# Two-layer decoder trunk on one core: the residual stream is laid out with tokens on partitions, and the out and down projections stream 512 weight columns

## The chip, the core and the metric

The kernel runs on one core of a Trainium2 chip. The core has five engines that run their own instruction streams and meet at semaphores: TensorE (PE, with its weight loads shown as PEld), VectorE (DVE), ScalarE (ACT), GpSimd (POOL) and SyncE (SP), which here issues DMAs. The metric is the device time of one execution in microseconds.

## What is computed

A trunk of two layers over 256 tokens of 1024 channels, all in float32. Each layer normalizes, mixes tokens in three ways, adds to the residual stream x, normalizes again, runs a gated MLP with a short convolution over positions, and adds to x; a closing norm ends it.

```python
D_MODEL = 1024; SEQ = 256; DEPTH = 2; D_FF = 2816

def rms_norm(x, g):
    y = xf * lax.rsqrt(jnp.mean(xf * xf, axis=-1, keepdims=True) + RMS_EPS)
    return y.astype(x.dtype) * g
...
    for i in range(DEPTH):
        h = rms_norm(x, norm_mix_g[i])
        x = x + hybrid_mixer(h, ..., w_branch[i], b_gate[i], w_out[i])
        h = rms_norm(x, norm_ffn_g[i])
        x = x + conv_ffn(h, w_up[i], ffn_conv_w[i], ffn_conv_b[i], w_down[i])
    return rms_norm(x, norm_f_g)
```

The two products that write the residual stream are the out projection (1024 x 1024 weights, the end of `hybrid_mixer`) and the down projection (2816 x 1024, the end of `conv_ffn`).

## The kernel before

**Float32 as two parts.** Every operand is split into a high part in a reduced format (fp32r) and the low rest; a product is three TensorE products, high x high, low x high and high x low, added up in PSUM. Activations are split by `split_scaled` (L290): ScalarE writes the high part times the norm's gain (L292), VectorE the low part (L293), into `slot_h` and `slot_l`.

**Weights.** They come from memory in 302 pieces, most of 128 x 1024 numbers (512 KB). `piece` (L157) loads one (L166, on SyncE's queue, four raw buffers), ScalarE casts it to `whi` (L173), VectorE subtracts to get `wlo` (L174); six buffers hold the two parts, and pieces are prepared `LOOK` = 5 ahead of their use. A dictionary `before` holds other loads that go into SyncE's queue ahead of a piece.

**Main stream and side tasks.** `stream()` runs the layers; the large products follow one another on TensorE, and a generator gives way after each step of some products. The token mixers and the factor of a norm are side tasks: `spawn` starts one, and it says how many steps of the main stream to wait before it goes on (the tables `N` and `W`). The framework's scheduler then fixes the order on each engine.

**Residual stream.** `xT` is [128, 8, 256]: channel 128 k + p of all tokens is row p of block k. A product that writes it has 128 weight columns as the stationary operand and streams the 256 tokens: `chan_steps` (L207; products at L217 to L219) for the out projection, `add_down` (L946; L954 to L956) for the down projection, which runs `FFN_LAG` = 3 tiles behind the up projection. Four PSUM banks `dacc` collect the down projection over its 22 tiles of 128 hidden channels. `take` (L914) and `add_x` (L979) add a bank to `xT` on VectorE. As soon as two blocks of `xT` are new, `Norm.part` splits them for the next product and squares them (L309), and GpSimd adds up the squares (L311).

**A norm's factor.** The factor of a token, 1 / rms, isn't needed for the next product, only for what takes its result. `Norm.factor` adds the squares' halves on GpSimd (L320), sums over channels by four products of TensorE with a single streamed column (L324), does a Newton iteration of small operations on VectorE (`rsqrt`, L271), makes a diagonal matrix `dg` (L331), and spreads it over partitions by another product (L334) into `r_bc`.

**Closing norm.** `Final` (L339) squares each pair of blocks when it is done (L349), adds them up (L351, L358), sums over channels on TensorE (L362), iterates (L274 to L279), spreads the factor (L369, L370), and scales the eight blocks on VectorE (L372), with five output DMAs (L376).

## Time and profile before

| | |
|---|---|
| median of 3 runs | 946.69 us (945.66 to 948.6) |
| span of the profiled execution | 946.7 us |
| TensorE busy | 931.4 us, 7258 products |
| VectorE busy | 715.4 us |
| ScalarE busy | 511.2 us |
| GpSimd busy | 96.5 us |
| moved by DMA | 165.45 MB, mean 175 GB/s |

Times are microseconds from the start of the span. A busy TensorE isn't necessarily a TensorE at its peak: its products are pipelined, and a product's shown duration is longer than the step from its start to that of the next. The step is what a product costs in a stream of products. An idle time in brackets names what ended it.

### The profile page before, as it was taken

What the parts mean: (1) busy time and instruction counts of PE and PEld (TensorE: products, weight loads), DVE (VectorE), ACT (ScalarE), POOL (GpSimd) and SP (SyncE); (2) the same over time, 40 slices, a digit from 0 to 9 for tenths busy, and PEclk for the clock granted to TensorE, in tenths of its full rate; (3) what the DMA queues carried; (4) which work ended last, traced back from release to release, by engine and by line L of the source; (5) the groups of instructions that cost most, each with busy time, mean ns of one, the idle gap of its engine ahead of it and who ended that gap; (6) DMA issues with size and microseconds to landing.
All of it is one profiled execution on the core that took longest, in us unless ns stands there. A gap on an engine that the chain in (4) does not pass through costs nothing.

```text
span 946.7 us, 18084 instructions
## 1 busy us (share of the span) xinstructions
PE 931.4 (98%) x7258; PEld 897.3 (95%) x7258; DVE 715.4 (76%) x1105; ACT 511.2 (54%) x755; POOL 96.5 (10%) x88
## 2 busy tenths in 40 slices
PE   8999999999999999999999999999999999999995
PEld 8899899899999999999999998989999999999995
DVE  6986888575578877777799578877657897777775
ACT  6665454554466555555557645544544575555541
POOL 3022200002120000000022031000202200000000
PEclk9999999999999999999999999999999999999998
DMA  7674665445565656665456556545565666666521
GB/s 236 215 230 130 233 187 164 142 153 180 172 196 166 200 179 181 182 189 183 145 181 183 171 166 216 154 149 147 173 189 169 181 193 182 182 187 188 178 91 45
DMA packets 49428, 165.45 MB, mean 175 GB/s; under 512 B 5760, under 2 KB 8384, under 8 KB 49344
## 3 DMA queue, kind: packets, MB, share of 16 engines
q1 hardware_dynamic: 49056, 163.90, 56.6%
q8 instruction: 57, 0.93, 0.4%
q10 hardware_dynamic: 288, 0.39, 0.1%
q14 instruction: 27, 0.22, 0.1%
HBM read 161.12 MB, written 1.05 MB: 171 GB/s over the span
## 4 chain that ended last, share of the span: by engine, by line
PE 92%; DMA 2%; DVE 2%; ACT 2%; issue 1%; SPq 0%; DVEq 0%; ACTq 0%
PE mm L217 21%; PE mm L218 20%; PE mm L219 20%; PE mx L955 4%; PE mx L954 4%; PE mx L956 4%; PE mm L264 4%; PE mm L265 4%; PE mm L266 3%; DMA raw<-w_all 2%; PE mx L486 2%; ACT whi L173 1%; PE mx L489 1%; DVE wlo L174 1%; PE mx L473 1%
## 5 line engine op out<-in xcount | busy, mean ns | idle before, releaser
L217 PE MATMUL mm<-slot_h,whi 128*128 128x256 f32 x1696 | 484.4, 286 | 1.4 <-ACT slot_h L292 1.4
L218 PE MATMUL mm<-slot_l,whi 128*128 128x256 f32 x1696 | 481.3, 284 | 0.6 <-DVE slot_l L293 0.6
L219 PE MATMUL mm<-slot_h,wlo 128*128 128x256 f32 x1696 | 481.0, 284 | 0.0
L174 DVE TENSOR_TENSOR wlo<-raw,whi 128x1024 fp32r<-128x1024 f32 (+1 forms) x300 | 376.0, 1255 | 113.3 <-ACT whi L173 109.9
L173 ACT CAST whi<-raw 128x1024 fp32r<-128x1024 f32 (+1 forms) x302 | 311.2, 1033 | 262.5 <-PE mm L218 163.0
L217 PEld LDWEIGHTS mm<-slot_h,whi 128*128 128x128 f32 x1696 | 326.2, 193 | 4.1 <-ACT slot_h L292 2.1
L218 PEld LDWEIGHTS mm<-slot_l,whi 128*128 128x128 f32 x1696 | 326.5, 193 | 1.5 <-DVE slot_l L293 1.2
L219 PEld LDWEIGHTS mm<-slot_h,wlo 128*128 128x128 f32 x1696 | 326.4, 192 | 0.1
L954 PE MATMUL mx<-slot_h,whi 128*128 128x256 f32 x346 | 97.9, 283 | 0.0
L955 PE MATMUL mx<-slot_l,whi 128*128 128x256 f32 x346 | 97.9, 283 | 0.0
L956 PE MATMUL mx<-slot_h,wlo 128*128 128x256 f32 x346 | 97.9, 283 | 0.0
L937 DVE SCALAR_TENSOR_TENSOR tm<-tm,par 128x254 f32<-128x254 f32 (+1 forms) x176 | 73.8, 477 | 0.7 <-ACT tm L935 0.7
L954 PEld LDWEIGHTS mx<-slot_h,whi 128*128 128x128 f32 x346 | 66.4, 192 | 0.0
L955 PEld LDWEIGHTS mx<-slot_l,whi 128*128 128x128 f32 x346 | 66.4, 192 | 0.0
L956 PEld LDWEIGHTS mx<-slot_h,wlo 128*128 128x128 f32 x346 | 66.4, 192 | 0.0
L264 PE MATMUL mm<-whi,slot_h 128*128 128x512 f32 x160 | 63.5, 397 | 0.2 <-DVE tm L408 0.2
L265 PE MATMUL mm<-wlo,slot_h 128*128 128x512 f32 x160 | 63.1, 394 | 0.0
L266 PE MATMUL mm<-whi,slot_l 128*128 128x512 f32 x160 | 62.5, 392 | 0.0
L935 ACT ACTIVATE tm<-tm,par 128x256 f32<-128x256 f32 x88 | 48.2, 593 | 4.1 <-DVE tm L930 4.0
L930 DVE TENSOR_TENSOR tm<-mm,r_bc 128x512 f32<-128x512 f32 x44 | 30.4, 690 | 22.1 <-PE mm L219 22.1
L941 ACT CAST slot_h<-tm 128x256 fp32r<-128x256 f32 x44 | 17.8, 406 | 50.7 <-DVE tm L940 50.7
L311 POOL TENSOR_TENSOR sqacc<-sqacc,tm 128x512 f32<-128x512 f32 x12 | 17.3, 1441 | 234.8 <-ACT tm L309 234.5
(197 smaller groups left out, 784.0 us busy)
## 6 DMA issues: line engine op xcount, KB each, us to landing
raw<-w_all SPq DMA_DIRECT2D x292, 512.0 KB, 3.6
st<-ret_decay SPq DMA_DIRECT2D x8, 384.0 KB, 4.1
raw<-w_all SPq DMA_DIRECT2D x10, 256.0 KB, 4.6
xT<-x_t SPq DMA_DIRECT2D x4, 256.0 KB, 7.0
r_c<-q SPq DMA_DIRECT2D x16, 64.0 KB, 2.1
r_d<-q SPq DMA_DIRECT2D x16, 64.0 KB, 2.1
r_a<-phases SPq DMA_DIRECT2D x2, 256.0 KB, 4.1
out_dram<-xT SPq DMA_DIRECT2D x2, 256.0 KB, 2.0
```

Of the source, the lines that this page charges most:

```text
L173: nc.scalar.copy(h_out, r_in)
L174: nc.vector.tensor_tensor(l_out, r_in, h_out.bitcast(F32), ALU.subtract)
L217: nc.tensor.matmul(o, lhsT=wh[:, c], rhs=ah[:, k, :], start=first, stop=False)
L218: nc.tensor.matmul(o, lhsT=wh[:, c], rhs=al[:, k, :], start=False, stop=False)
L219: nc.tensor.matmul(o, lhsT=wl[:, c], rhs=ah[:, k, :], start=False, stop=last)
L264: nc.tensor.matmul(acc[t], lhsT=ah[:, k, c], rhs=wh, start=first, stop=False)
L265: nc.tensor.matmul(acc[t], lhsT=ah[:, k, c], rhs=wl, start=False, stop=False)
L266: nc.tensor.matmul(acc[t], lhsT=al[:, k, c], rhs=wh, start=False, stop=last)
L937: nc.vector.scalar_tensor_tensor(a[:, d:], u[:, :T - d], mx.pc("fconv_w", 3 * ct + 2 - d), a[:, d:], ALU.mult, ALU.add)
L954: nc.tensor.matmul(o, lhsT=wh[:, c], rhs=ah[:, a, :], start=(first and i == 0), stop=False)
L955: nc.tensor.matmul(o, lhsT=wh[:, c], rhs=al[:, a, :], start=False, stop=False)
L956: nc.tensor.matmul(o, lhsT=wl[:, c], rhs=ah[:, a, :], start=False, stop=end)
```

## The change

The residual stream becomes `xt`, [128, 2, 1024]: token 128 t + p is row p of token tile t. The out projection (`tok_major`, one half of 512 channels after the other) and the down projection (`add_down` by half c and token tile t) now have 128 tokens of the activations as the stationary operand and stream 512 weight columns. Per layer that is 96 products for the out projection in place of 192, and 264 for the down projection in place of 528. The weights of the out projection lie in memory in another order for this.

The sum of squares of a token now lies along its row: `grow` adds a half bank to `xt` and squares it with ScalarE's accumulator (`ss`). No sums over partitions are left except in layer 0's first norm (`FirstNorm`), which still loads a channel-major copy of x into two borrowed buffers. The next product, though, needs channels on partitions, so `TokNorm.turn` transposes a half on TensorE (eight 128 x 128 blocks) into PSUM and splits from there. `DOWN_END` and `CLOSE_END` give the order of the last entries of the down projection (tiles from the end, half, token tile). The closing norm multiplies by a broadcast gain (on GpSimd for three of the four quarters, on VectorE for the last), iterates for each token tile, and scales along rows. New loads are x by tokens (1 MB, ahead of an early piece) and the gain of the closing norm (512 KB, in layer 1).

The core of the diff (comments and the packing of inputs left out):

```diff
FFN_LAG = 3
-DOWN_LAG = 2.5
+DOWN_END = ((3, 0, 0), (2, 0, 0), (3, 0, 1), (2, 0, 1), (3, 1, 0), (2, 1, 0), (1, 0, 0), (1, 0, 1),
+            (3, 1, 1), (2, 1, 1), (1, 1, 0), (1, 1, 1))
+CLOSE_END = ((3, 0, 0), (2, 0, 0), (3, 1, 0), (2, 1, 0), (4, 0, 1), (3, 0, 1), (1, 0, 0), (1, 1, 0),
+             (4, 1, 1), (3, 1, 1), (2, 1, 1), (2, 0, 1), (1, 0, 1), (1, 1, 1))
...
 REST = 9
...
-N = (3, 8, 4, 5, 1)
+N = (3, 8, 3, 5, 3, 2)
...
+X_AT = 40
...
-    def tok_major(l, kind, act):
+    def tok_major(l, kind, act, half=0):
         ah, al = act
         acc = [mm_tile() for _ in range(2)]
         for k in range(KT):
-            wh, wl = weight(l, kind, k // 4, k % 4, 512)
+            wh, wl = weight(l, kind, 2 * half + k // 4, k % 4, 512)
             for t in range(2):
                 c = slice(t * P, (t + 1) * P)
                 first, last = k == 0, k == KT - 1
...
     class Norm:
         def __init__(self, g, slot):
             self.g, self.slot = g, slot
+            self.r_bc = None
+        def spread(self, src):
+            r = rsqrt(src, 2, 1.0 / D, 1e-6)
+            rh = sm.tile([P, 2], F32, name="rh", tag="rh")
+            nc.vector.tensor_scalar(rh, r, 0.5, None, ALU.mult)
+            dg = sm.tile([P, T], F32, name="dg", tag="sq1", bufs=1)
+            for t in range(2):
+                nc.vector.tensor_scalar(dg[:, t * P:(t + 1) * P], ident, r[:, t:t + 1], None, ALU.mult)
+            yield self.late
+            pb = mx_tile()
+            nc.tensor.matmul(pb[:, :T], lhsT=ones[:, :P], rhs=dg, start=True, stop=True)
+            r_bc = sm.tile([P, T], F32, name="r_bc", tag="r_bc", bufs=1)
+            nc.scalar.copy(r_bc, pb[:, :T])
+            self.r, self.rh, self.r_bc = r, rh, r_bc
+    class FirstNorm(Norm):
+        late = N[1]
+        def __init__(self, g, slot):
+            super().__init__(g, slot)
             self.acc = sm.tile([P, 512], F32, name="sqacc", tag="sqacc", bufs=1)
-            self.r_bc = None
-        def split(self, j):
-            for k in (2 * j, 2 * j + 1):
-                split_scaled(self.slot[0][:, k, :], self.slot[1][:, k, :], xT[:, k, :], self.g[:, k:k + 1])
+            self.x = [mix.tile([P, 4, T], F32, name="x_t", tag=q) for q in ("m_lo", "m_hi")]
+        def ahead(self, j):
+            o = 2 * (j % 2)
+            x = self.x[j // 2][:, o:o + 2, :]
+            nc.sync.dma_start(x, xT_in[:, 2 * j:2 * j + 2, :])
+            for i in range(2):
+                k = 2 * j + i
+                split_scaled(self.slot[0][:, k, :], self.slot[1][:, k, :], x[:, i, :], self.g[:, k:k + 1])
         def square(self, j):
             sq = self.acc if j == 0 else t_main()
-            nc.scalar.activation(two(sq), xT[:, 2 * j:2 * j + 2, :], AF.Square)
+            o = 2 * (j % 2)
+            nc.scalar.activation(two(sq), self.x[j // 2][:, o:o + 2, :], AF.Square)
             if j:
                 nc.gpsimd.tensor_tensor(self.acc, self.acc, sq, ALU.add)
-        def part(self, blocks):
-            j = blocks[0] // 2
-            self.split(j)
-            self.square(j)
         def factor(self):
             s1 = sm.tile([P, T], F32, name="sq1", tag="sq1", bufs=1)
...
             for t in range(2):
                 nc.tensor.matmul(pv[:, t:t + 1], lhsT=s1[:, t * P:(t + 1) * P], rhs=ones[:, 0:1],
                                  start=(t == 0), stop=(t == 1))
...
+            yield from self.spread(pv[:, 0:2])
+    def grow(ss, c, t, acc):
+        x = xt[:, t, 512 * c:512 * c + 512]
+        nc.vector.tensor_tensor(x, x, acc, ALU.add)
+        sq = t_main()
+        nc.scalar.activation(sq, x, AF.Square, accum_out=ss[:, 2 * c + t:2 * c + t + 1])
+        return x
+    class TokNorm(Norm):
+        late = N[4]
+        def __init__(self, g, slot):
+            super().__init__(g, slot)
+            self.ss = sm.tile([P, 4], F32, name="xss", tag="xss")
+        def add(self, c, t, acc):
+            grow(self.ss, c, t, acc)
+        def turn(self, c):
+            for q in (2 * c, 2 * c + 1):
+                pt = mx_tile()
+                for j in range(2):
+                    for t in range(2):
+                        nc.tensor.transpose(pt[:, j * T + t * P:j * T + (t + 1) * P],
+                                            xt[:, t, (2 * q + j) * P:(2 * q + j + 1) * P], ident)
+                for j in range(2):
+                    k = 2 * q + j
+                    split_scaled(self.slot[0][:, k, :], self.slot[1][:, k, :], pt[:, j * T:(j + 1) * T],
+                                 self.g[:, k:k + 1])
+        def turn_late(self, c):
+            self.turn(c)
+            yield 1
+        def factor(self):
+            s2 = sm.tile([P, 2], F32, name="xs2", tag="xs2")
+            nc.vector.tensor_tensor(s2, self.ss[:, 0:2], self.ss[:, 2:4], ALU.add)
+            yield from self.spread(s2)
     class Final:
         def __init__(self):
...
+            self.g = mix.tile([P, D], F32, name="fin_g", tag="m_lo")
+            nc.sync.dma_start(self.g, fin)
+            self.ss = sm.tile([P, 4], F32, name="xss", tag="xss")
+        def add(self, c, t, acc):
+            x = grow(self.ss, c, t, acc)
+            eng = nc.vector if c == t == 1 else nc.gpsimd
+            eng.tensor_tensor(x, x, self.g[:, 512 * c:512 * c + 512], ALU.mult)
+        def finish(self, t):
+            s1 = sm.tile([P, 1], F32, name="xs1", tag="xs2")
+            nc.vector.tensor_tensor(s1, self.ss[:, t:t + 1], self.ss[:, 2 + t:3 + t], ALU.add)
+            r = rsqrt(s1, 1, 1.0 / D, 1e-6)
+            for c in range(2):
+                x = xt[:, t, 512 * c:512 * c + 512]
+                if c:
+                    nc.vector.tensor_scalar(x, x, r, None, ALU.mult)
+                    nc.sync.dma_start(out[:, t, 512 * c:512 * c + 512], x)
+                else:
+                    nc.scalar.activation(x, x, AF.Copy, scale=r)
+                    nc.scalar.dma_start(out[:, t, 512 * c:512 * c + 512], x)
...
     def layer(l, norm):
         mx = Mixers(l, norm)
         x_act = slots[0]
+        if l:
+            spawn(norm.turn_late(1), N[5])
         factor = spawn(norm.factor(), N[2] if l else N[3])
         def take(b, acc):
...
         finish(gla)
         yield from branch(2, gts)
...
+        norm = TokNorm(mx.pc("ffn_g", 0, 8), slots[1])
+        for c in range(2):
+            acc = yield from tok_major(l, "out", slots[0], c)
+            for t in range(2):
+                norm.add(c, t, acc[t])
+            spawn(norm.turn_late(c), N[5])
+            if c == 0:
+                yield
         fx = slots[1]
         ah, al = slots[2]
         dacc = []
...
             nc.scalar.copy(ah[:, j % 4, :], cv[:, :T])
             nc.vector.tensor_tensor(al[:, j % 4, :], cv[:, :T], ah[:, j % 4, :].bitcast(F32), ALU.subtract)
...
+        def add_down(k, c, t, first, last):
+            wh, wl = (a[:, 512 * c:512 * c + 512] for a in weight(l, "down", k, 0, D))
+            o, a, tok = dacc[2 * c + t], k % 4, slice(t * P, (t + 1) * P)
+            nc.tensor.matmul(o, lhsT=ah[:, a, tok], rhs=wh, start=first, stop=False)
+            nc.tensor.matmul(o, lhsT=ah[:, a, tok], rhs=wl, start=False, stop=False)
+            nc.tensor.matmul(o, lhsT=al[:, a, tok], rhs=wh, start=False, stop=last)
+        closing = l + 1 == L
+        end = [(NF - b, c, t) for b, c, t in (CLOSE_END if closing else DOWN_END)]
+        factor = spawn(norm.factor(), N[2])
         def take(j, acc):
             finish(factor)
...
             if j >= FFN_LAG:
                 if not dacc:
                     dacc += [mx_tile() for _ in range(4)]
...
+                for c in range(2):
+                    for t in range(2):
+                        if (j - FFN_LAG, c, t) not in end:
+                            add_down(j - FFN_LAG, c, t, j == FFN_LAG, False)
+        nxt = Final() if closing else TokNorm(params[l + 1][:, PO["mix_g"]:PO["mix_g"] + 8], slots[0])
+        for n, (k, c, t) in enumerate(end):
+            last = k == NF - 1
+            add_down(k, c, t, False, last)
+            if last:
+                nxt.add(c, t, dacc[2 * c + t])
+                if closing and c:
+                    nxt.finish(t)
+            elif not closing and (c, t) == (1, 1) and k == NF - 3:
+                nxt.turn(0)
         return nxt
     def stream():
-        norm = Norm(params[0][:, PO["mix_g"]:PO["mix_g"] + 8], slots[0])
+        norm = FirstNorm(params[0][:, PO["mix_g"]:PO["mix_g"] + 8], slots[0])
         cold = mx_tile()
         for _ in range(WARM):
             nc.tensor.matmul(cold[:, :T], lhsT=ones[:, :P], rhs=ones, start=True, stop=True)
-        def x_ahead(j):
-            nc.sync.dma_start(xT[:, 2 * j:2 * j + 2, :], xT_in[:, 2 * j:2 * j + 2, :])
-            norm.split(j)
         def rest_ahead():
             nc.sync.dma_start(cs, cst)
...
             for l in range(1, L):
                 nc.sync.dma_start(params[l], par[l])
-        before.update({q + 1: lambda j=q: x_ahead(j) for q in range(4)})
+        before.update({q + 1: lambda j=q: norm.ahead(j) for q in range(4)})
+        before[X_AT] = lambda: nc.sync.dma_start(xt, x_in)
         before[REST] = rest_ahead
         nc.sync.dma_start(params[0], par[0])
         piece(0)
         for l in range(L):
             norm = yield from layer(l, norm)
-        norm.finish()
     for _ in stream():
         for task in list(tasks):
...
```

Where the halves of the out projection are taken up in layer 0, VectorE's queue before (names: `raw`, `whi`, `wlo` a weight piece and its parts, `mm` and `mx` PSUM banks):

```order
L462 SCALAR_TENSOR_TENSOR slot_l_88<-m_hi,slot_h_87 128x512
L174 TENSOR_TENSOR wlo<-raw,whi 128x1024 x2
L914 TENSOR_TENSOR xT<-xT,mm 128x512
L174 TENSOR_TENSOR wlo<-raw,whi 128x1024
L293 SCALAR_TENSOR_TENSOR slot_l_90<-xT,par_74,slot_h_89 128x256 x2
```

and now:

```order
L510 SCALAR_TENSOR_TENSOR slot_l_88<-m_hi,slot_h_87 128x512
L180 TENSOR_TENSOR wlo<-raw,whi 128x1024 x3
L361 TENSOR_TENSOR xt<-xt,mm 128x512 x2
L180 TENSOR_TENSOR wlo<-raw,whi 128x1024
L299 SCALAR_TENSOR_TENSOR slot_l_90<-mx,par_74,slot_h_89 128x256 x4
```

Four additions with a pair of low parts behind each have become two pairs of additions with four low parts behind each pair. On TensorE the transposes of the first half stand behind six products of the second half, which is here:

```order
L270 MATMUL mm<-whi,slot_h_87 128x512
L271 MATMUL mm<-wlo,slot_h_87 128x512
L272 MATMUL mm<-whi,slot_l_88 128x512
L384 MATMUL mx<-cs,xt 128x128 x8
L270 MATMUL mm<-whi,slot_h_87 128x512
```

Eight transposes have come between the products of one bank. At the change of layer, VectorE's queue before:

```order
L979 TENSOR_TENSOR xT<-xT,mx 128x512
L174 TENSOR_TENSOR wlo<-raw,whi 128x1024 x2
L293 SCALAR_TENSOR_TENSOR slot_l_88<-xT,par_75,slot_h_87 128x256 x2
L979 TENSOR_TENSOR xT<-xT,mx 128x512 x2
L293 SCALAR_TENSOR_TENSOR slot_l_88<-xT,par_75,slot_h_87 128x256 x2
```

and now:

```order
L361 TENSOR_TENSOR xt<-xt,mx 128x512 x2
L180 TENSOR_TENSOR wlo<-raw,whi 128x1024
L299 SCALAR_TENSOR_TENSOR slot_l_88<-mx,par_75,slot_h_87 128x256
L361 TENSOR_TENSOR xt<-xt,mx 128x512
L180 TENSOR_TENSOR wlo<-raw,whi 128x1024
L299 SCALAR_TENSOR_TENSOR slot_l_88<-mx,par_75,slot_h_87 128x256 x2
```

The low parts now wait for transposes (`mx`) and are spread among additions and weight splits. At the end of the kernel, VectorE's queue before (two more rounds of the iteration, the spread and the eight scalings follow):

```order
L979 TENSOR_TENSOR xT<-xT,mm 128x256 x2
L358 TENSOR_TENSOR tm<-tm 128x256 x3
L274 TENSOR_SCALAR rs_v<-mm 128x2
L275 TENSOR_SCALAR rs_y<-rs_v 128x2
L277 TENSOR_TENSOR rs_a<-rs_y 128x2
L278 SCALAR_TENSOR_TENSOR rs_a<-rs_a,rs_v 128x2
L279 SCALAR_TENSOR_TENSOR rs_y<-rs_a,rs_y 128x2
```

and now, from the first token tile's last small operation:

```order
L285 SCALAR_TENSOR_TENSOR rs_y<-rs_a,rs_y 128x1
L361 TENSOR_TENSOR xt<-xt,mx 128x512
L420 TENSOR_SCALAR xt<-xt,rs_y 128x512
L361 TENSOR_TENSOR xt<-xt,mx 128x512
L411 TENSOR_TENSOR xt<-xt,fin_g 128x512
L415 TENSOR_TENSOR xs_10206<-xss 128x1
```

The first tile's iteration stands ahead of the second tile's additions, and eleven more small operations and one scaling (L420) follow the last row.

## Rows read from the trace of the kernel before

**Rows 1.** The page: busy us (share of the span) and instructions of each engine.

```profile
PE 931.4 (98%) x7258; PEld 897.3 (95%) x7258; DVE 715.4 (76%) x1105; ACT 511.2 (54%) x755; POOL 96.5 (10%) x88
```

**Rows 2.** Layer 0's MLP: PE, PEld, DVE, ACT, POOL busy, clock, DMA share, GB/s.

```profile
286.00:470.00 184.00, 184.00 (x1535) 183.95 (x1534) 146.08 (x233) 102.82 (x152) 0.74 (x1) 1.00 0.60 182
```

**Rows 3.** Timeline of TensorE (start, duration): products with 256 columns, 24 steps.

```profile
700.04 0.28 PE L217 MATMUL mm<-slot_h,whi 128*128 128x256 f32 x1
...
702.92 0.28 PE L217 MATMUL mm<-slot_h,whi 128*128 128x256 f32 x1
```

**Rows 4.** Timeline of TensorE: products with 512 columns, eleven steps.

```profile
111.64 0.39 PE L264 MATMUL mm<-whi,slot_h 128*128 128x512 f32 x1
...
114.13 0.39 PE L266 MATMUL mm<-whi,slot_l 128*128 128x512 f32 x1
```

**Rows 5.** Timeline of TensorE: four transposes in the mixers.

```profile
201.83 0.60 PE L473 MATMUL mx<-cs,tx 128*128 128x128 f32 x4
...
202.39 0.28 PE L218 MATMUL mm<-slot_l,whi 128*128 128x256 f32 x1
```

**Rows 6.** Timeline of TensorE: the sums of a norm.

```profile
287.64 0.50 PE L324 MATMUL mx<-ones,sq 128*128 128x1 f32 x4
...
288.21 0.28 PE L218 MATMUL mm<-slot_l,whi 128*128 128x256 f32 x1
```

**Rows 7.** Groups by line and shape: count, busy us, mean ns, idle before.

```profile
L174 DVE TENSOR_TENSOR wlo<-raw,whi 128x1024 fp32r<-128x1024 f32 x292 | 367.9, 1262 | 110.8 <-ACT whi L173 107.6
L173 ACT CAST whi<-raw 128x1024 fp32r<-128x1024 f32 x292 | 305.3, 1047 | 261.2 <-PE mm L218 163.0 <-PE mx L955 31.9 <-issue 25.4
...
L293 DVE SCALAR_TENSOR_TENSOR slot_l<-mx,par,slot_h 128x256 fp32r<-128x256 f32 x24 | 10.8, 479 | 3.7 <-ACT slot_h L292 3.7
...
L979 DVE TENSOR_TENSOR xT<-xT,mx 128x512 f32<-128x512 f32 x8 | 5.4, 684 | 5.9 <-PE mx L956 5.9
```

**Rows 8.** Timeline of TensorE at the change of layer.

```profile
472.82 0.52 PE L217 MATMUL mm<-slot_h,whi 128*128 128x256 f32 x3
...
473.92 0.38 PE L218 MATMUL mm<-slot_l,whi 128*128 128x256 f32 x1 [0.57 <-DVE slot_l L293]
```

**Rows 9.** Timeline some 16 us later: TensorE at the spread of the factor.

```profile
489.07 0.28 PE L217 MATMUL mm<-slot_h,whi 128*128 128x256 f32 x1
...
489.58 0.67 PE L334 MATMUL mx<-dg,ones 128*128 128x256 f32 x2 [0.24 <-DVE dg L331]
```

**Rows 10.** A window in the start of layer 0, columns as in rows 2.

```profile
30.00:32.00 2.00, 2.00 (x15) 1.78 (x13) 2.00 (x7) 0.47 (x1) 0.00 (x0) 1.00 0.89 309
```

**Rows 11.** Timeline of that stretch's longest wait: VectorE beside GpSimd, then TensorE.

```profile
54.54 2.02 DVE L174 TENSOR_TENSOR wlo<-raw,whi 128x1024 fp32r<-128x1024 f32 x1 [0.26 <-ACT whi L173]
...
55.44 2.02 POOL L532 TENSOR_TENSOR sg_d<-sg_c,dt 128x512 f32<-128x512 f32 x1
...
56.48 1.08 DVE L515 TENSOR_TENSOR da<-dt,aneg 128x8 f32<-128x8 f32 x2
...
57.54 0.39 PE L524 MATMUL mx<-da,cs 128*128 128x8 f32 x2 [1.33 <-DVE da L515]
```

**Rows 12.** Timeline of the tail.

```profile
933.29 1.28 POOL L351 TENSOR_TENSOR tm<-tm 128x512 f32<-128x512 f32 x1 [185.55 <-ACT tm L349]
933.30 0.69 DVE L979 TENSOR_TENSOR xT<-xT,mx 128x512 f32<-128x512 f32 x1 [0.75 <-PE mx L956]
...
933.70 0.28 PE L956 MATMUL mm<-slot_h,wlo 128*128 128x256 f32 x1
...
934.09 1.24 ACT L349 ACTIVATE tm<-xT 128x512 f32<-128x512 f32 x3 [0.87 <-DVE xT L979]
...
936.73 0.16 DVE L274 TENSOR_SCALAR rs_v<-mm 128x2 f32<-128x2 f32 x1 [0.76 <-PE mm L362]
...
938.70 0.16 DVE L279 SCALAR_TENSOR_TENSOR rs_y<-rs_a,rs_y 128x2 f32<-128x2 f32 x1
...
940.56 3.22 DVE L372 SCALAR_TENSOR_TENSOR xT<-xT,par,mm 128x256 f32<-128x256 f32 x8 [1.18 <-PE mm L370]
```

More of the change, by code (lines that the diff above doesn't have):

```diff
@@ L50 @@
 _at = 0
-for _n, _w in (("mix_g", 8), ("ffn_g", 8), ("fin_g", 8), ("b_gate", 24), ("conv_w", 24), ("conv_b", 6),
+for _n, _w in (("mix_g", 8), ("ffn_g", 8), ("b_gate", 24), ("conv_w", 24), ("conv_b", 6),
                ("ssm_g", 4), ("ret_g", 4), ("gla_g", 4), ("b_alpha", 2), ("fconv_w", 132), ("fconv_b", 44),
@@ L118, in hybrid_trunk @@
 @with_exitstack
-def hybrid_trunk(ctx: ExitStack, tc: tile.TileContext, xT_in, wall, par, wa2, cst, phase, dret, out):
+def hybrid_trunk(ctx: ExitStack, tc: tile.TileContext, xT_in, x_in, wall, par, wa2, cst, phase, dret, fin, out):
     nc = tc.nc
@@ L127, in hybrid_trunk @@
     ps = ctx.enter_context(tc.tile_pool(name="ps", bufs=4, space=PSUM))
-    xT = cpool.tile([P, KT, T], F32, name="xT")
+    xt = cpool.tile([P, 2, D], F32, name="xt")
     params = [cpool.tile([P, NP], F32, name=f"par{l}") for l in range(L)]
@@ L325, in factor @@
                                  start=(t == 0), stop=(t == 1))
-            r = rsqrt(pv[:, 0:2], 2, 1.0 / D, 1e-6)
-            rh = sm.tile([P, 2], F32, name="rh", tag="rh")
-            nc.vector.tensor_scalar(rh, r, 0.5, None, ALU.mult)
-            dg = sm.tile([P, T], F32, name="dg", tag="sq1", bufs=1)
-            for t in range(2):
-                nc.vector.tensor_scalar(dg[:, t * P:(t + 1) * P], ident, r[:, t:t + 1], None, ALU.mult)
-            yield N[1]
-            pb = mx_tile()
@@ L334, in factor @@
-            nc.tensor.matmul(pb[:, :T], lhsT=ones[:, :P], rhs=dg, start=True, stop=True)
-            r_bc = sm.tile([P, T], F32, name="r_bc", tag="r_bc", bufs=1)
-            nc.scalar.copy(r_bc, pb[:, :T])
-            self.r, self.rh, self.r_bc = r, rh, r_bc
+            yield from self.spread(pv[:, 0:2])
[5 more added lines that the diff above has]
+        return x
@@ L907, in layer @@
         yield from branch(2, gts)
-        norm = Norm(mx.pc("ffn_g", 0, 8), slots[1])
-        def take(j, acc):
-            xp = xT[:, 2 * j:2 * j + 2, :]
-            nc.vector.tensor_tensor(xp, xp, two(acc), ALU.add)
-            norm.part((2 * j, 2 * j + 1))
-        yield from chan_two(l, "out", (0, 1), slots[0], take)
-        for j in (2, 3):
-            acc = yield from chan_major(l, "out", j, slots[0])
-            take(j, acc)
-            yield
+        norm = TokNorm(mx.pc("ffn_g", 0, 8), slots[1])
[6 more added lines that the diff above has]
+                yield
         fx = slots[1]
@@ L942, in activate @@
             nc.vector.tensor_tensor(al[:, j % 4, :], cv[:, :T], ah[:, j % 4, :].bitcast(F32), ALU.subtract)
-        groups = [(0, 1), (2, 3), (4, 5), (6, 7)]
-        def add_down(k, first, last, which):
-            wh, wl = weight(l, "down", k, 0, D)
-            a = k % 4
-            for g in which:
-                for i, b in enumerate(groups[g]):
-                    o = dacc[g][:, i * T:(i + 1) * T]
-                    c = slice(b * P, (b + 1) * P)
-                    end = last and i == len(groups[g]) - 1
-                    nc.tensor.matmul(o, lhsT=wh[:, c], rhs=ah[:, a, :], start=(first and i == 0), stop=False)
-                    nc.tensor.matmul(o, lhsT=wh[:, c], rhs=al[:, a, :], start=False, stop=False)
-                    nc.tensor.matmul(o, lhsT=wl[:, c], rhs=ah[:, a, :], start=False, stop=end)
-        factor = spawn(norm.factor(), N[4])
+        def add_down(k, c, t, first, last):
[7 more added lines that the diff above has]
+        factor = spawn(norm.factor(), N[2])
         def take(j, acc):
@@ L1061, in _lay_weights @@
             elif kind == "out":
-                put(l, kind, j, i["w_out"][l][:, 256 * j:256 * j + 256])
+                put(l, kind, j, i["w_out"][l][512 * (j % 2):512 * (j % 2) + 512, 512 * (j // 2):512 * (j // 2) + 512])
             elif kind == "up":
@@ L1082, in _lay_params @@
         put(l, "ffn_g", cols(i["norm_ffn_g"][l]))
-        put(l, "fin_g", cols(i["norm_f_g"]))
         put(l, "b_gate", cols(i["b_gate"][l].reshape(-1)))
@@ L1139 @@
     got = r.results[0]["out_0_dram"]
-    return np.ascontiguousarray(got.transpose(2, 1, 0).reshape(1, T, D))
+    return np.ascontiguousarray(got.transpose(1, 0, 2).reshape(1, T, D))
```

54 lines of the change are left out of this document (3 added, 51 removed).

## Prediction

> **What bounds the kernel now.** I read the page first, then the timeline of TensorE at places where one kind of product runs undisturbed, then the places where TensorE waits. TensorE is busy for 931.4 of 946.7 us, 98% [rows 1]; in the 184 us of the first layer's MLP it is busy throughout, while VectorE has 146 us of work, ScalarE 103, and the DMAs move 182 GB/s [rows 2]. So time is what TensorE's instructions take, plus a few places where it stands still: the start of layer 0, the change of layer, and the tail behind the last product. The granted clock is 1.00 in that window, the upper level (2.4 GHz), and nothing here gives a reason for it to change.
>
> The profiled execution spans 946.7 us and the median of the three runs is 946.69, so a difference in the span is used as a difference in the time, unscaled. A measurement of this kernel tells about 0.3% (2.84 us) from no change.
>
> **Products.** A product with 256 columns starts 0.120 us after the one before it: 24 steps from 700.04 to 702.92 [rows 3]. One with 512 takes 0.226 to 0.227: 11 steps from 111.64 to 114.13 [rows 4]. Two of the short for one of the long saves 2 x 0.120 - 0.227 = 0.013 us. Out projection, both layers: 2 x (192 x 0.120 - 96 x 0.227) = 2.50 us. Down projection: 2 x (528 x 0.120 - 264 x 0.227) = 6.86. Together **-9.4**. The work is in the open: no other engine ends later in the MLP [rows 2]; a cycle of one MLP tile falls from 72 x 0.120 = 8.64 to 48 x 0.120 + 12 x 0.227 = 8.48 us, in which VectorE has 146.08 / 184 x 8.64 = 6.9 us of work.
>
> The Trainium skill ("TensorE: Matmul & The Clock Gate", Back-to-back issue gap) gives an isolated warm gap of N / 2.4 GHz + 2.5 ns, which is 109 and 216 ns, and thus saves only 2.5 ns per pair. The trace's 120 and 227 disagree with both figures, and the measurement is used.
>
> **Transposes and sums.** New are 48 transposes of 128x128: three norms (both MLP norms and the second layer's first) have eight blocks by two token tiles. Four such transposes in the mixers push the next step from 201.83 + 0.12 to 202.39: 0.44 us [rows 5], so 48 cost **+5.3**. Gone are the four 128x1 products of the sums at the same three norms, 0.45 us each time (287.64 to 288.21, less 0.12) [rows 6]: **-1.3**. Moved off the path: nine of the twelve GpSimd additions of squares, which are hidden today; I cost them at nothing. TensorE's own work is then -9.4 + 5.3 - 1.3 = **-5.4**.
>
> **Out to up projection** (twice). Today no product waits there. After the change the eight transposes of a half stand in TensorE's order behind only six products of the next half, 6 x 0.227 = 1.36 us. They need both residual additions, 2 x 0.68 [rows 7], which begin some 0.2 us after the last product: 1.6 us. The second half's transposes come after two steps of the up projection and have slack. Bounds: 0 to 1 us each time, the upper one if the weight split ahead of the additions in VectorE's queue (1.26 us [rows 7]) is late by most of its length. I take 0.15 each, **+0.3**. The slices of the operand then come from PSUM: 0.48 us each on VectorE, as the mixers' [rows 7], in a stretch where it has room.
>
> **Change of layer.** Today TensorE stalls twice: the low part of an operand comes 1.10 - 3 x 0.12 = 0.74 us late (472.82 to 473.92), because VectorE's subtraction stands behind two weight splits [rows 8], and the spread of the factor is waited for some 16 us later, 0.51 - 0.12 = 0.39 us [rows 9]. Both places keep the same shape: the low part still follows an addition and a weight split in VectorE's queue, but sixteen transposes and one more step (addition, transposes, cast, subtraction) lie before it; the products of the last blocks, now standing after the first transposes, cover most of that. Replaying the order with the durations of [rows 7] I get 0.9 us against 1.13: **-0.2**, bounds -1 to +2.
>
> **Start.** Layer 0's first norm keeps its channel-major x, so that part is unchanged, but 1 MB more (the token-major x) is put into SyncE's queue between two weight pieces near 30 us, where the DMAs already move 309 GB/s [rows 10]. That is 1.05 MB / 309 GB/s = 3.4 us of transfer ahead of the next piece. The raw buffers hold several pieces ahead, and TensorE's longest wait after it today is 1.33 us, for VectorE and not for a piece (57.54) [rows 11]. So I take **+0.5**, bounds 0 to +2. The gain row of the closing norm (512 KB) is loaded where TensorE has five pieces in hand, at nothing; uncovered it would be 1.7 us.
>
> **Tail.** Before: the last product starts at 933.70, so it is through at 933.82, and the span ends at 946.66: 12.84 us of squares, sums, a Newton iteration of 11 small operations (0.196 us from start to start), eight scalings over 3.22 us, and 2.88 us from the last scaling's end to the end [rows 12]. After, with zero at the end of the last product: the first token tile's entries end at -4.08 (six entries of three products of 0.227 follow them). Its second addition ends at -4.08 + 0.2 + 0.69 = -3.2, its square at -2.5 (1.24 us for a square of 512 and two of 256 [rows 12]; I take half, as for a single one of 512). Then 12 small VectorE operations, 2.35 us. But GpSimd now multiplies two quarters by the gain, 1.28 us each (the row at 933.29 [rows 12]), from -3.1 to -0.5. Half of the small operations read two operands from SBUF, and a two-operand VectorE instruction beside a GpSimd one is seen to wait: two of 128x8 elements took 1.08 us, until GpSimd's ended (55.44 + 2.02), and a weight split 2.02 us instead of 1.26 [rows 7, 11]. An addition from PSUM beside GpSimd took its usual 0.69 [rows 12]. So I let them end at +1.35 rather than -0.05. The order then fixes the rest: addition (2.05), scaling (0.6 for 512 elements, between 3.22 / 8 = 0.40 for 256 and the additions' 0.69: 2.65), last addition (3.35), its square (4.05, since ScalarE first scales the first tile), GpSimd's third multiplication until 4.5, VectorE's own (5.2), 12 small operations (7.55), scaling (8.15), and 2.88 for the transfer: 11.0, some 11.1 with hand-overs. **-1.7**; unblocked it is 9.2 (-3.6).
>
> For the blocking the Trainium skill has a rule ("SBUF — State Buffer", Who interferes with whom): a VectorE instruction with two SBUF inputs contends with a GpSimd instruction that reads SBUF. The trace agrees (1.08 us for two of 128x8); by the rule the tail is the 11.1, without it 9.2.
>
> **Sum.** -5.4 + 0.3 - 0.2 + 0.5 - 1.7 = -6.5: **940.2 us**.
>
> **The rivals.**
> - *The sum as it stands*, 940.2, between about 938.7 and 942.5 by the start and the hand-overs. Chance 0.50.
> - *The small operations slip between GpSimd's*: the weight splits of [rows 11] got through between two GpSimd operations. Tail -3.6 in place of -1.7: 938.3. Chance 0.22.
> - *New waits take the place of the sums.* Transposes are queued on TensorE behind VectorE additions at six points; the change of layer shows that two weight splits ahead in VectorE's queue cost 0.74 us [rows 8]. At that price in each of six it is 4.4 instead of the 0.3 taken: 944.3; with the upper bound of the start 945.8. Chance 0.17.
> - *Slower.* If at the turns a weight split stands before the addition and its buffer is released only by the product just ahead of the transposes, TensorE waits for its own release: cast 1.05 + split 1.26 + addition 0.68 + hand-overs 0.2 = 3.2 us [rows 7]. At all six turns that is 19 and 959 us, at three of them 9.6 and 950. It decides from 1.6 us a turn, (6.5 + 2.84) / 6. Against it: VectorE and ScalarE have room in the MLP [rows 2], and pieces are split five ahead. Chance 0.06.
> - *The longer columns save next to nothing*: if a long product costs two short ones in the new places (0.240 us) or a fifth of the 0.013 less, the 9.4 us shrink to between 0 and 1.9 and the time is 949.6 to 947.7, no change. The two steps of [rows 3, 4] come from the same kernel and the same kinds of operands, which speaks against it. Chance 0.05. The isolated gap of the Trainium skill's page named above belongs here: by an estimate from it 720 pairs save 1.8 us, and the time would be 947.8.
>
> **How the numbers follow.** Faster by over 0.3% is below 943.85: 0.49 from the first case, 0.22 from the second, 0.06 from the third (where some turns wait and others don't): 0.77. Within 0.3%: 0.01, 0.11 from the third and 0.05 from the last: 0.17. Slower than 949.53: the fourth: 0.06. The range of 8 in 10 leaves out the best end of the second case, the fourth and fifth, and the upper end of the third: 936.3 to 945.6.
>
> **What will show it.** Right: 512-column products at 0.227 us in the down projection; VectorE's addition rows 0.69; 48 transposes at 0.11 us; a tail from the last product of 9 to 11 us with the small operations stretched where GpSimd multiplies. Wrong: a stall of over 1 us in TensorE's timeline ahead of the transposes; a wait of TensorE between 30 and 58 us much above 1.33; granted clock below 1.00 in the MLP.

## The result, and the profile after

The changed kernel takes 939.34 us (median of 4 runs, 937.93 to 940.86) against 946.2 for the kernel before; the ratio is 0.9921 with a 95% interval of 0.9902 to 0.9941. That is 7 us less, as forecast (940.2 us, faster by over 0.3%).

The page after, busy us and instructions of each engine, then the chain that ended last [rows 1]:

```profile
PE 921.8 (98%) x6558; PEld 858.5 (91%) x6558; DVE 707.3 (75%) x1109; ACT 512.4 (55%) x772; POOL 82.8 (9%) x78
...
PE 92%; DVE 3%; DMA 2%; ACT 2%; issue 1%; SPq 0%; ACTq 0%; DVEq 0%
```

There are 700 products fewer: 720 went in the out and down projections (96 + 264 in each layer), 12 with the sums of three norms and 16 with the closing norm, and 48 transposes came. TensorE is still the chain.

**Where the time went.** The starts of a few products cut both timelines into stages that hold the same work (us from one landmark to the next; the first landmark is the product at L568 before and L616 after, the second half of the mixer's first scores):

| stage, up to | before | after | difference |
|---|---|---|---|
| first score product of the state space mixer, layer 0 | 69.36 | 68.25 | -1.11 |
| last mixer product, layer 0 | 120.67 | 120.66 | 0 |
| first down product (the out projection lies in it) | 115.76 | 115.86 | +0.10 |
| last down product, layer 0 | 166.92 | 164.60 | -2.32 |
| last mixer product, layer 1 (the change of layer lies in it) | 178.32 | 177.72 | -0.60 |
| first down product, layer 1 | 115.76 | 115.86 | +0.10 |
| last down product, layer 1 | 166.92 | 163.68 | -3.24 |
| end of the span | 12.96 | 11.66 | -1.30 |

The first row can't be counted as gain, since the start varies by 2.5 us between the profiles below; the other seven add up to -7.26 us. Layer 0's stage up to the last down product gains less than layer 1's because the first eight transposes for layer 1 lie in it.

The last products of the down projection after, TensorE's timeline [rows 3, 4]:

```profile
922.10 0.39 PE L993 MATMUL mx<-whi,slot_h 128*128 128x512 f32 x1
...
926.63 0.39 PE L995 MATMUL mx<-whi,slot_l 128*128 128x512 f32 x1
```

Twenty steps in 4.53 us, 0.2265 each, the step that 512 columns had before. The granted clock in both spans is 0.996.

Out to up projection, VectorE and TensorE after (there was nothing like it before):

```profile
265.25 3.50 DVE L180 TENSOR_TENSOR wlo<-raw,whi 128x1024 fp32r<-128x1024 f32 x3 [0.25 <-ACT whi L179]
268.66 1.28 DVE L361 TENSOR_TENSOR xt<-xt,mm 128x512 f32<-128x512 f32 x2
```

```profile
268.41 0.39 PE L272 MATMUL mm<-whi,slot_l 128*128 128x512 f32 x1
...
269.77 0.39 PE L272 MATMUL mm<-whi,slot_l 128*128 128x512 f32 x1
270.00 1.03 PE L384 MATMUL mx<-cs,xt 128*128 128x128 f32 x8
270.79 0.48 PE L270 MATMUL mm<-whi,slot_h 128*128 128x512 f32 x1
```

The last product of the first half starts at 268.41. The first addition starts at 268.66, as VectorE's third weight split ends (268.75): its bank, the first token tile's, was complete three products before. The two additions are through at 269.94: 0.06 us before TensorE comes to the transposes at 270.00. No time is lost, with next to no reserve.

The change of layer after, TensorE and VectorE [rows 8, 9]:

```profile
469.37 0.39 PE L995 MATMUL mx<-whi,slot_l 128*128 128x512 f32 x1
469.60 0.28 PE L223 MATMUL mm<-slot_h,whi 128*128 128x256 f32 x1
469.72 0.28 PE L224 MATMUL mm<-slot_l,whi 128*128 128x256 f32 x1
...
480.00 0.28 PE L224 MATMUL mm<-slot_l,whi 128*128 128x256 f32 x1
480.37 0.70 PE L318 MATMUL mx<-dg,ones 128*128 128x256 f32 x2
```

```profile
467.92 1.22 DVE L180 TENSOR_TENSOR wlo<-raw,whi 128x1024 fp32r<-128x1024 f32 x1 [1.08 <-ACT whi L179]
469.06 0.48 DVE L299 SCALAR_TENSOR_TENSOR slot_l<-mx,par,slot_h 128x256 fp32r<-128x256 f32 x1
```

The first low part is done at 469.54, and the first product that reads one starts at 469.72 on its step: the wait of 0.74 us is gone, and that for the spread factor has fallen from 0.39 to 0.37 - 0.12 = 0.25.

The tail after, GpSimd, VectorE, ScalarE and the last DMA issue [rows 12]:

```profile
923.82 2.56 POOL L411 TENSOR_TENSOR xt<-xt,fin_g 128x512 f32<-128x512 f32 x2 [202.03 <-ACT tm L363]
```

```profile
924.46 0.68 DVE L415 TENSOR_TENSOR xs<-xss 128x1 f32<-128x1 f32 x1 [0.79 <-ACT tm L363]
925.17 0.15 DVE L280 TENSOR_SCALAR rs_v<-xs 128x1 f32<-128x1 f32 x1
...
925.55 0.84 DVE L283 TENSOR_TENSOR rs_a<-rs_y 128x1 f32<-128x1 f32 x1
926.43 0.16 DVE L284 SCALAR_TENSOR_TENSOR rs_a<-rs_a,rs_v 128x1 f32<-128x1 f32 x1
...
927.87 0.68 DVE L361 TENSOR_TENSOR xt<-xt,mx 128x512 f32<-128x512 f32 x1
...
930.58 1.24 DVE L411 TENSOR_TENSOR xt<-xt,fin_g 128x512 f32<-128x512 f32 x1 [1.05 <-ACT tm L363]
...
934.05 0.49 DVE L420 TENSOR_SCALAR xt<-xt,rs_y 128x512 f32<-128x512 f32 x1
```

```profile
934.11 0.72 ACT L423 ACTIVATE xt<-xt,rs_y 128x512 f32<-128x512 f32 x1 [3.56 <-DVE rs_y L285]
934.86 0.34 ACTq L424 DMA_DIRECT2D out_dram<-xt  x1
```

One number for each partition takes 0.68 and 0.84 us where GpSimd multiplies, and 0.15 to 0.16 elsewhere; the two ends (925.14 and 926.39) are those of GpSimd's two operations to 0.02 us. VectorE's own multiplication takes 1.24 instead of 0.68. From the last product's start to the end it is 11.66 us, 12.96 before.

### The profile page after: what moved, and what is told of

Read it like the earlier page. It is cut to its first block, busy times and chain, and to the rows that moved or that the text cites. A ratio compares the mean times of both kernels' runs of the same rounds, so it can differ in the third digit from the quotient of the medians.

```text
span 938.3 us, 16691 instructions
## 1 busy us (share of the span) xinstructions
PE 921.8 (98%) x6558; PEld 858.5 (91%) x6558; DVE 707.3 (75%) x1109; ACT 512.4 (55%) x772; POOL 82.8 (9%) x78
## 4 chain that ended last, share of the span: by engine, by line
PE 92%; DVE 3%; DMA 2%; ACT 2%; issue 1%; SPq 0%; ACTq 0%; DVEq 0%
PE mm L223 19%; PE mm L224 19%; PE mm L225 19%; PE mm L270 5%; PE mm L271 5%; PE mm L272 5%; PE mx L993 4%; PE mx L994 4%; PE mx L995 4%; PE mx L534 2%; DMA raw<-w_all 1%; DVE wlo L180 1%; PE mx L537 1%; PE mx L521 1%; DMA x_t<-x_t 1%
## 5 line engine op out<-in xcount | busy, mean ns | idle before, releaser
L223 PE MATMUL mm<-slot_h,whi 128*128 128x256 f32 x1568 | 447.1, 285 | 1.4 <-ACT slot_h L298 1.4
L224 PE MATMUL mm<-slot_l,whi 128*128 128x256 f32 x1568 | 444.1, 283 | 0.4 <-DVE slot_l L299 0.2
L225 PE MATMUL mm<-slot_h,wlo 128*128 128x256 f32 x1568 | 444.0, 283 | 0.1
L983 DVE SCALAR_TENSOR_TENSOR tm<-tm,par 128x255 f32<-128x255 f32 (+1 forms) x176 | 73.5, 478 | 0.7 <-ACT tm L981 0.7
L993 PE MATMUL mx<-whi,slot_h 128*128 128x512 f32 x176 | 69.1, 392 | 0.0
L994 PE MATMUL mx<-wlo,slot_h 128*128 128x512 f32 x176 | 69.0, 392 | 0.0
L995 PE MATMUL mx<-whi,slot_l 128*128 128x512 f32 x176 | 68.5, 389 | 0.0
L270 PEld LDWEIGHTS mm<-whi,slot_h 128*128 128x128 f32 x224 | 42.1, 188 | 8.8 <-issue 0.3
L272 PEld LDWEIGHTS mm<-whi,slot_l 128*128 128x128 f32 x224 | 42.1, 188 | 8.7
L271 PEld LDWEIGHTS mm<-wlo,slot_h 128*128 128x128 f32 x224 | 42.1, 188 | 8.3
```

Of the source, the lines that this page charges most:

```text
L223: nc.tensor.matmul(o, lhsT=wh[:, c], rhs=ah[:, k, :], start=first, stop=False)
L224: nc.tensor.matmul(o, lhsT=wh[:, c], rhs=al[:, k, :], start=False, stop=False)
L225: nc.tensor.matmul(o, lhsT=wl[:, c], rhs=ah[:, k, :], start=False, stop=last)
L270: nc.tensor.matmul(acc[t], lhsT=ah[:, k, c], rhs=wh, start=first, stop=False)
L271: nc.tensor.matmul(acc[t], lhsT=ah[:, k, c], rhs=wl, start=False, stop=False)
L272: nc.tensor.matmul(acc[t], lhsT=al[:, k, c], rhs=wh, start=False, stop=last)
```

## Experiments

All are edits of the changed kernel, but for a repeat of each kernel. Times are medians; the kernel before had 946.8 us beside the first four, 947.3 beside the next four, and 946.8 beside the last two. Stages are those of the table above.

**256 columns in the down projection.**

```diff
-            nc.tensor.matmul(o, lhsT=ah[:, a, tok], rhs=wh, start=first, stop=False)
...
+            for h in range(2):
+                q = slice(256 * h, 256 * h + 256)
+                nc.tensor.matmul(o[:, q], lhsT=ah[:, a, tok], rhs=wh[:, q], start=first and h == 0, stop=False)
...
```

> The changed kernel, but the down projection streams its weights in two halves of 256 columns: 528 products a layer in place of 264, tokens still on partitions. If the longer columns are the gain (0.227 to 0.229 us for 512 against 2 x 0.120 in the two traces), it takes 528 x (0.240 - 0.229) to 528 x (0.240 - 0.227) = 5.8 to 6.9 us more than the changed kernel, some 945.5. The rival, that the columns save next to nothing and the gain lies in waits that went away: within 1.5 us of the changed kernel's 939.3.

946.03 us, ratio to the kernel before 0.9995 (0.9985 to 1.0005): 6.7 us more than the changed kernel. The two stages with the down projection take 167.84 and 166.92, 3.24 more each: 3.24 / 264 = 0.0123 us for each pair. The columns are the gain: with those of the down projection taken back, the rest of the change (costs and savings that nearly cancel) can't be told from nothing.

**256 columns in the out projection.**

```diff
-                nc.tensor.matmul(acc[t], lhsT=ah[:, k, c], rhs=wh, start=first, stop=False)
...
+                for h in range(2 if kind == "out" else 1):
+                    q = slice(256 * h, 256 * h + 256) if kind == "out" else slice(0, 512)
...
+                    nc.tensor.matmul(acc[t][:, q], lhsT=ah[:, k, c], rhs=wh[:, q], start=first and h == 0, stop=False)
...
```

> The changed kernel, but the out projection streams its weights in halves of 256 columns: 192 products a layer in place of 96. Longer columns as the cause: 192 x 0.010 to 192 x 0.013 = 2.0 to 2.5 us more, some 941.6, the same products' steps at 0.120 in the trace. Rival: no difference in the stretch between the last branch product and the first product of the up projection.

943.28 us, ratio 0.9957 (0.9941 to 0.9974). The stage with the out projection takes 117.06 in both layers, 1.20 more: 1.20 / 96 = 0.0125 for each pair, 2.4 us in all, as expected. The rest of the 3.9 us between the medians isn't in any later stage; it is no more than the start varies.

**Every transpose twice.**

```diff
-                        nc.tensor.transpose(pt[...], xt[...], ident)
+                        for _ in range(2):
+                            nc.tensor.transpose(pt[...], xt[...], ident)
```

> The changed kernel with every new transpose made twice, 96 in place of 48. If the transposes lie in the open and nothing is waited for in front of them, 48 x 0.094 to 48 x 0.110 = 4.5 to 5.3 us more than the changed kernel, some 944.2. If TensorE waits at the turns anyway (for additions or for what the transposes feed), the second transposes cost less in the first case or more in the second: below 3 or above 7 us.

944.53 us, ratio 0.997 (0.9958 to 0.9982): 5.2 more. Sixteen transposes more in the stage with the out projection cost 117.61 - 115.86 = 1.75 us, 0.109 each, in both layers. Of the sixteen more at the change of layer, the eight in the stage before the last down product cost 0.96, the other eight 0.55: behind them TensorE no longer waits for the spread factor (0.25 us in the changed kernel).

**Without GpSimd's multiplications.**

```diff
-            eng = nc.vector if c == t == 1 else nc.gpsimd
-            eng.tensor_tensor(x, x, self.g[:, 512 * c:512 * c + 512], ALU.mult)
+            if c == t == 1:
+                nc.vector.tensor_tensor(x, x, self.g[:, 512 * c:512 * c + 512], ALU.mult)
```

> The changed kernel without GpSimd's three multiplications by the closing gain (three quarters of the output lack the gain); everything else stands in the same order. If GpSimd blocks VectorE's two-operand instructions, the first iteration loses 0.53 + 0.68 us of waiting (its end is then set by the product that it follows: addition at 926.75 in place of 927.87) and VectorE's own multiplication takes 0.68 in place of 1.24: the tail falls from 11.4 to some 9.7 us, the time by 1.7. Rival, that the order of VectorE and ScalarE alone sets the tail: 11.4 and no difference.

937.08 us, ratio 0.9896 (0.9877 to 0.9914). The order on VectorE is the same, the tail 9.96 us: 1.70 less. VectorE's timeline:

```profile
926.00 0.68 DVE L361 TENSOR_TENSOR xt<-xt,mx 128x512 f32<-128x512 f32 x1
...
928.72 0.69 DVE L411 TENSOR_TENSOR xt<-xt,fin_g 128x512 f32<-128x512 f32 x1 [1.04 <-ACT tm L363]
929.33 0.15 DVE L415 TENSOR_TENSOR xs<-xss 128x1 f32<-128x1 f32 x1
```

The multiplication takes 0.69 us again, and no small operation is stretched. GpSimd's blocking is shown, and its size at this place.

**The load of x late.**

```diff
-        before[X_AT] = lambda: nc.sync.dma_start(xt, x_in)
+        def x_late():
+            nc.scalar.copy(xt[:, 0, 0:1], loaded[X_AT - 1][0][:, 0:1].bitcast(F32))
+            nc.sync.dma_start(xt, x_in)
+        before[X_AT] = x_late
```

with `X_AT` = 64.

> The changed kernel, but the load of the token-major x (1 MB) waits for the cast of a weight piece in the middle of layer 0 (by a copy of one column that ScalarE writes into its target), in place of standing between two pieces near 30 us. If that load costs the start the 0.5 us of the prediction (0 to 2), the median falls by that, and the stretch up to the first score product of the state space mixer, 68.25 us in the changed kernel and 67.6 to 68.8 in the four kernels with the same start, comes to some 67.5. If the load is covered, no difference beyond 0.6 us either way.

940.83 us, ratio 0.9921 (0.9906 to 0.9936), and the unchanged kernel beside it 939.77. The start takes 69.13. The load where it stands costs nothing that can be seen in the time, but it isn't hidden. It is issued at 29.89 us in the changed kernel; ScalarE then waits for a weight piece, and TensorE behind it:

```profile
35.15 1.05 ACT L179 CAST whi<-raw 128x1024 fp32r<-128x1024 f32 x1 [1.24 <-DMA raw<-w_all]
...
42.02 0.61 PE L550 MATMUL mx<-pick,small 128*128 128x8 f32 x4 [1.12 <-DVE small L472]
...
55.22 0.39 PE L572 MATMUL mx<-da,cs 128*128 128x8 f32 x2 [0.43 <-DVE da L563]
```

With the load late there is no such wait near 42 us, but the later wait is as long as the 1.33 us before [rows 11]:

```profile
55.81 0.39 PE L572 MATMUL mx<-da,cs 128*128 128x8 f32 x2 [1.31 <-DVE da L563]
```

The wait near 42 us, 0.5 to 1.7 us, stands in seven of the nine profiles with the load in its place near 30 us and in none of the three others; the later one is under 0.5 us in all nine. Why the later wait shrinks was not tested.

**Transposes at once.**

```diff
-N = (3, 8, 3, 5, 3, 2)
+N = (3, 8, 3, 5, 3, 0)
```

> The changed kernel, but the transposes of a half are spawned without the wait of two steps. In the order, two products of the next half stand ahead of the first half's transposes in place of six, and twelve products of the up projection ahead of the second half's in place of twenty-four. If the wait for the additions is what those products cover, TensorE stands still for some 1.58 - 2 x 0.227 = 1.1 us at each out projection's first half and up to 0.2 at its second: 2.2 to 3 us more in all, in the stretch from the last mixer product to the first down product (115.86 us in both layers). Rival, that the additions are through well before: less than 0.5 us.

940.81 us, ratio 0.9931 (0.9916 to 0.9945). The stage with the out projection takes 116.24 and 116.23, 0.38 more each, 0.76 in all: a miss, between the two theories. The edit also reaches the second half's transposes at the change of layer; that stage takes 0.12 more. TensorE's timeline:

```profile
268.67 0.39 PE L271 MATMUL mm<-wlo,slot_h 128*128 128x512 f32 x1
...
269.21 0.44 PE L384 MATMUL mx<-cs,xt 128*128 128x128 f32 x2 [0.16 <-DVE xt L361]
```

TensorE does wait for the addition, for 0.54 - 0.23 = 0.3 us. But the transposes of one token tile need one addition alone, the first half's first tile is complete three products (0.68 us) before the second, and the scheduler set two transposes ahead and six behind two further products. The 1.1 us expected took both additions as due before the first transpose.

**Another closing norm.**

```diff
-            x = grow(self.ss, c, t, acc)
-            eng = nc.vector if c == t == 1 else nc.gpsimd
-            eng.tensor_tensor(x, x, self.g[:, 512 * c:512 * c + 512], ALU.mult)
+            grow(self.ss, c, t, acc)
...
+        def end(self, t, r):
             for c in range(2):
                 x = xt[:, t, 512 * c:512 * c + 512]
...
+                nc.vector.scalar_tensor_tensor(x, x, r, self.g[:, 512 * c:512 * c + 512], ALU.mult, ALU.mult)
+                (nc.scalar, nc.sync)[c].dma_start(out[:, t, 512 * c:512 * c + 512], x)
...
-                    nxt.finish(t)
+                    if t == 0:
+                        r0 = nxt.begin(0)
+                    else:
+                        nxt.end(0, r0)
+                        nxt.end(1, nxt.begin(1))
```

> The changed kernel with another closing norm, with the same result: no multiplication by the gain on GpSimd; VectorE multiplies by factor and gain in one operation for each quarter, for the first token tile in the time in which it waits for the second tile's squares. By the durations of the changed kernel: iteration of the first tile to 926.8, additions and two scalings to 929.6, the second tile's iteration from 929.8 to 932.15, two scalings of 0.7 to 933.5, 3.44 from the last DMA issue to the end: 937 in place of 938.3, the tail from the last product's start 10.3 in place of 11.66 us. If GpSimd's blocking is not what holds VectorE, the two scalings more on VectorE make it no shorter than 11.66.

937.74 us, ratio 0.9899 (0.9884 to 0.9915): faster than both kernels. The tail is 9.78 us, 1.88 less than in the changed kernel (and 0.5 less than expected). VectorE's first small operation for the second token tile, and the last two scalings:

```profile
928.59 0.16 DVE L413 TENSOR_TENSOR xs<-xss 128x1 f32<-128x1 f32 x1 [0.18 <-ACT tm L363]
...
930.91 1.41 DVE L419 SCALAR_TENSOR_TENSOR xt<-xt,rs_y,fin_g 128x512 f32<-128x512 f32 x2
```

Factor and gain in one operation take 0.7 us for a quarter, against 0.49 for the factor alone; the multiplications on GpSimd and the wait that they brought are saved.

**The changed kernel again.**

> The changed kernel once more, unchanged, beside these. If what differs from run to run lies in the start alone, every stage from the first score product on takes the same as in the first profile to 0.1 us (120.66, 115.86, 164.60, 177.7, 115.86, 163.68, 11.66), the start 67.5 to 69, and the median 939.3.

939.77 us, ratio 0.9921 (0.9904 to 0.9937). Stages from the first score product on: 120.68, 115.86, 164.58, 177.68, 115.86, 163.68, 11.68. The start took 66.88 us, 1.4 less than in the first profile: what varies from run to run lies there, as far as these profiles show.

**The first half's transposes later at the change of layer.**

```diff
-            elif not closing and (c, t) == (1, 1) and k == NF - 3:
+            elif not closing and (c, t) == (1, 1) and k == NF - 2:
                 nxt.turn(0)
```

> The changed kernel, but the first half's transposes at the change of layer stand three products later. In VectorE's order two weight splits then stand ahead of the first low parts, as in the kernel before, in place of one. If that is what made TensorE stand still for 0.74 us there before (and its absence what gave most of the 1.0 us more than forecast at this place), the first product with a low part waits 0.5 to 1.6 us, and the stretch from the last down product of layer 0 to the last mixer product of layer 1, 177.7 us in the changed kernel, takes some 178.7. Rival, that the tokens' layout itself took the wait away: 177.7.

940.59 us, ratio 0.9935 (0.9915 to 0.9955). The stage takes 178.57, 0.85 more; the others are unchanged. VectorE, TensorE and ScalarE:

```profile
467.60 2.36 DVE L180 TENSOR_TENSOR wlo<-raw,whi 128x1024 fp32r<-128x1024 f32 x2 [1.08 <-ACT whi L179]
469.88 0.87 DVE L299 SCALAR_TENSOR_TENSOR slot_l<-mx,par,slot_h 128x256 fp32r<-128x256 f32 x2
```

```profile
469.04 0.40 PE L995 MATMUL mx<-whi,slot_l 128*128 128x512 f32 x1
469.55 0.62 PE L223 MATMUL mm<-slot_h,whi 128*128 128x256 f32 x3
470.41 0.38 PE L224 MATMUL mm<-slot_l,whi 128*128 128x256 f32 x1 [0.25 <-DVE slot_l L299]
```

```profile
469.04 0.82 ACT L298 ACTIVATE slot_h<-mx,par 128x256 fp32r<-128x256 f32 x2
```

With two weight splits ahead of the low parts the wait is back, 470.41 - 469.55 - 3 x 0.12 = 0.50 us, and TensorE starts the three products that need no low part first, as before the change. So the tokens' layout alone doesn't take the wait away; the place in VectorE's queue does. The edit did a second thing: the later transposes bring ScalarE's first high part later, and TensorE waits for that too, 469.55 - 469.04 - 0.23 = 0.28 us. The 0.85 us is not the price of the split alone.

**The kernel before again.**

> The kernel before once more. If the stages repeat to 0.1 us and only the start differs from run to run, the stages from the first score product on are 120.67, 115.76, 166.92, 178.32, 115.76, 166.92 and 12.96 us again, and the start is between 66 and 70 us; with a start below 69.36 the 1.1 us by which the first profiles differ there are no gain of the change.

946.76 us (one run); stages 120.66, 115.76, 166.92, 178.34, 115.76, 166.92, 12.96, and a start of 67.67. Over all twelve profiles the start lies between 66.9 and 69.4 us, for both kernels; the 69.36 that the prediction was made on is its upper end.

## Why the prediction was right, point by point

- **What bounds it, and the products.** Right. TensorE's stream decided, and a pair of short products for a long one gave 0.0123 to 0.0125 us by the two experiments, not 0.013: 720 pairs at 0.0124 are 8.9 us in place of 9.4. The unbroken run above has the step of 0.2265; among the 256-column products of layer 1's MLP (780 to 900 us) the steps from one long product to the next are 0.226 to 0.236, 0.229 on average. The rival of columns that save nothing falls with both: the down projection alone was worth 6.5 us. The isolated gap of the Trainium skill ("TensorE: Matmul & The Clock Gate", Back-to-back issue gap) would give, as an estimate from its formula, 528 x 0.0025 = 1.3 us for the down projection; the experiment decides against it.
- **Transposes and sums.** Right: 0.109 us for a transpose (0.110 forecast), except where TensorE would have waited anyway.
- **Out to up projection.** +0.3 forecast, 0 measured: the stage came out at +0.10, which is 1.75 for transposes less 1.2 for the products and 0.45 for the sums. The step that failed is the additions' start, 0.2 us after the last product's step in the prediction and 0.02 after it in the trace (268.66, against 268.41 + 0.23). The prediction hung the first addition on the half's last product; it needs the first token tile's bank alone, and what it waited for was the weight split ahead of it. The margin of 0.06 us shows that the place was rightly seen as tight, and the experiment with the transposes at once that TensorE waits there when the cover is taken away, though less than the prediction's way of counting gave. The rival of new waits at all turns, and the slower one, did not come.
- **Change of layer.** The largest miss among the waits: -0.2 forecast, -0.9 measured (0.74 + 0.39 before, 0.25 after). The prediction said that "both places keep the same shape" and that a low part still stands behind a weight split. One split stands there, not two, and the replay missed what that is worth: the experiment that puts the second back brings a wait of 0.50 us for the low part (0.85 for the stage, with the wait for the high part).
- **Start.** +0.5 forecast, no net cost seen. The load of 1 MB does reach TensorE, with 1.12 us near 42 us in the first profile, but the wait at 55 us is 0.43 instead of 1.33; the prediction had the first effect and not the second. A cost of 0.5 us either way is less than the start varies, so this term is not settled; the 1.1 us by which the profiled starts differ prove nothing. Here the base was also off: in all runs but one the time is 1.7 to 1.9 us above the span, so the span of 946.7 belonged to an execution of some 948.5 us, not to one of the median. The sum was of differences, so it stands.
- **Tail.** -1.7 forecast, -1.4 measured from the last product's end (12.84 to 11.44; the table counts from its start). Right in the mechanism: the blocking and the order came as replayed, 0.1 to 0.7 us sooner from the first iteration's end on, up to VectorE's last scaling, which ended at 934.54 (7.7 us after the last product, 8.15 forecast). The prediction took half of the small operations as reading two operands from SBUF; by the code of `rsqrt` and `finish` it is ten of twelve, but only the two that came up while GpSimd multiplied were held. The whole tail, 11.4 us, lies just outside the 9 to 11 that the prediction named as a sign. What was under-sized is the end: ScalarE's scaling of the other quarter takes 0.72 us and ends 0.29 after VectorE's, and its DMA ends 3.44 us after its issue, where the prediction put 2.88 after VectorE's last. Without GpSimd's work the tail is 9.7 us from the last product's end, near the 9.2 of the rival in which nothing is held. The rule of the Trainium skill ("SBUF — State Buffer", Who interferes with whom), that a VectorE instruction with two SBUF inputs contends with a GpSimd instruction that reads SBUF, holds in this trace: 0.68 and 0.84 us for one number a partition.

By stage, against the prediction's terms put into them: the stages with the out projection 0.10 for 0.21 (each), the MLPs -2.32 for -2.55 and -3.24 for -3.43, the change of layer -0.60 for 0.23, the tail -1.30 for -1.6 to -1.7, the start 0 for 0.5. Too much was forecast for the columns, the tail and the start, and too little for the waits that went; together -7.26 for -6.5. That the sum came this close owes something to misses of both signs, which is luck.

## What to carry to other kernels

Where TensorE is the chain, price its instructions by the step from start to start, for each shape, in the trace itself: two rows of before gave the gain of the columns to 6%. Then treat every hand-over as a queue: what stands ahead of the awaited operation on its engine decides the wait. With one weight split more ahead of a low part on VectorE, TensorE waited 0.50 us. An engine that is set to work in a latency-bound tail may hold up the one that sets its end; folding its work into an operation that was there anyway took 1.9 us off.

## What was not expected of the hardware

An accumulating square on ScalarE is followed by a separate read of the accumulator, 0.19 us each time (16 of them, mean 187 ns). The holding of VectorE was forecast, but not how small an operation it takes: one on two operands of one number for each partition was held until GpSimd's multiplication had ended, 0.84 us in place of 0.16, while one-operand operations beside the same multiplication took their 0.15.
